# Two layers of experts in six rounds of 128 slots instead of eight, the places ranked by counts, w1 and w3 loaded two rows to a partition

## The chip, the core and the metric

The kernel runs on one core of a Trainium2 chip. A core has a matrix engine (TensorE, PE in the rows, with its weight loads as PEld), VectorE (DVE), ScalarE (ACT), GpSimd (POOL) and SyncE (SP); on SP stand the transfers from memory that this text is about. The engines have queues of their own and wait for each other through semaphores. The metric is the device time of one execution in microseconds, the median of several runs.

## The reference

A model of two blocks for 256 tokens of 1024 features, in float32. The first block has two layers; each is a mixing layer of four kinds of attention and then a mixture of experts. The second block has feed-forward, mLSTM and Mamba sublayers, which the change doesn't touch. The mixture of experts, cut to what matters:

```python
def _hier_moe(x, w_group, b_group, w_expert, b_expert, w1, w3, w2):
    g_sel = argmax(x @ w_group + b_group)                # one of 4 groups
    e_logits = (x @ w_expert + b_expert)[group g_sel]    # its 4 experts
    top_logit, top_idx = lax.top_k(e_logits, 2)
    gate = softmax(top_logit) * softmax(g_logits)[g_sel]
    ...
    h = silu(xb @ w1[e]) * (xb @ w3[e])                  # 1024 -> 512
    y = h @ w2[e]                                        # 512 -> 1024
    ...
    return sum over the two experts of a token of gate * y
```

So 256 tokens make 512 assignments to 16 experts, 32 per expert on average, and each layer needs all of w1, w3 and w2: 16 experts of 6.3 MB.

## The kernel before

**Work of a stage.** After the mixing layer, `route` (L977) works out for each token tile t (128 tokens) the two experts, the gates G and `pos`, each assignment's number among those of its expert. `moe` (L1066) then gives every expert 64 slots. A one-hot matrix `Ds` (tokens by slots, `dispatch` L1035) multiplies x, kept as two parts xh and xl, into `xe`, the slots' tokens transposed. The experts go by twos: a round p works on 128 slots, 64 of one expert and 64 of the other, so there are eight rounds. `up(p)` multiplies the slots of `xe` with w1 and then with w3, the two experts in the two column halves of TensorE (128\*64), four steps of two blocks of 128 features each; ScalarE and VectorE make h = silu(.) * (.). `down(p)` transposes h to hT, multiplies by w2 in four steps, and multiplies the result, scaled by the gate (yh and yl), with CT, the transpose of Ds, into four accumulators. The loop runs up(p) and then down(p - 1). Every second round starts with a dispatch of four experts; `collect` makes CT and the gates of eight.

**The fuller expert.** `count` (L1120), in the middle of up(0), sums the counts, and `place_fullest` (L1041) lets the fullest of experts 4 to 15 change places with the one at place TWICE = 11. That expert has 64 more slots: its pieces of w1, w3 and w2 are kept in `kept`, `select` (L1254) collects 64 more tokens after up(4), `more_up` (L1290) multiplies them after up(5), and `more_down` (L1314) follows after down(5). Assignments beyond that go into a loop behind the stage (`overflow` L1331), which runs nj times, 64 assignments each, and loads the expert's weights again.

**Weights.** `load_w` (L239) loads pieces of 512 KB, [128 partitions, h, n]. For w1 and w3 (n = 512) partition p gets rows p and p + 128 of a piece, for w2 (n = 1024) one row. An expert has four pieces each of w1, w3 and w2. `experts` (L910) yields the loads in the order of use: w1 and w3 of round p, then w2 of round p - 1. SP issues all of them in this order. A piece needs a slot of SBUF: there are 36 of 4 KB per partition (`take`, `give`), which hold everything else of that size too, and a load waits until the slot's last reader is done. The mixing layer loads ahead until 14 slots are left (`prefetch`). From expert 4 on the expert of a place is known on the chip alone: SP reads it from `who`, which place_fullest writes.

All matmuls of experts go through `mm` (L188), those of dispatch and the like through a bank's `mm` (L112). A float32 matmul is two instructions in the trace.

Of the kernel before, what the change touches and what calls it, by code (L numbers as in the profile page):

```python
# [12 lines left out]
F32R = mybir.dt.float32r  # L13
# [3 lines left out]
OP = mybir.AluOpType  # L17
# [3 lines left out]
P = 128  # L21
# [26 lines left out]
def _consts():  # L48
# [15 lines left out]
    addf("slots", np.broadcast_to(np.arange(64) + 1.0, (P, 64)))  # L64
    pos = np.arange(256, dtype=np.float32)
# [39 lines left out]
class Bank:  # L105
    """a PSUM bank that several products share as one accumulation group"""
# [18 lines left out]
class K:  # L125
# [89 lines left out]
    def copy(self, out, in_, eng=None):  # L215
        """PSUM or SBUF to SBUF, the two engines in turn."""
# [5 lines left out]
    def rstd(self, ss, scale, eps, n=1):  # L222
        """(ss * scale + eps) ** -0.5"""
# [7 lines left out]
    def rsqrt_sum(self, ss, n):  # L231
        """(ss[0] + ss[1] + n * EPS) ** -0.5: the reciprocal root mean square, over n ** 0.5"""
# [6 lines left out]
    def load_w(self, src, kt, n):  # L239
        """[kt*128, n] of DRAM, in pieces [128, h, n] of at most 512 KiB: [(first k, h, what loads it)]"""  # L240
# [28 lines left out]
    def held_back(self, eng):  # L269
        """on ScalarE or VectorE: not before what self.holds names, [how many, behind what] after each other"""  # L270
# [6 lines left out]
    def mm3(self, out, l, r, start, stop):  # L277
        """(lh + ll) (rh + rl) but for ll*rl"""
# [7 lines left out]
    def pieces(self, w, scale=None):  # L286
        """split one after the other"""
# [5 lines left out]
    def xk(self, xT, k, t=None):  # L293
        """(hi, lo) of block k of an x^T, of one token tile or both"""
# [3 lines left out]
    def rows_t(self, sp, xT, out, t, lo_last=False):  # L298
        """out = x_t @ w for one token tile; w in split pieces [128, h, n]"""
# [11 lines left out]
    def dense_rows(self, w, xT, outs):  # L311
        """outs[t] = x_t @ w for both token tiles, piece by piece"""
# [6 lines left out]
    def acc_t(self, sp, xT, acc, t, first=True, last=True):  # L319
        """acc[t][half] (+)= x_t @ w; w in split pieces [128, h, 1024]"""  # L320
# [7 lines left out]
    def dense_cols(self, w, blocks, xT):  # L328
        """for (bank, out, c, n) in blocks: out [n, 256] = (x @ w[:, c:c+n])^T"""
# [10 lines left out]
    def make_xT(self, rows, t, xT, kt=KT, r=None, k0=0, mod=None, bank=None, hold=None):  # L340
        """rows [128, kt*128] -> blocks k0 to k0 + kt of xT, token tile t, times r (of rows); mod: times and plus columns"""
# [31 lines left out]
    def load_params(self):  # L373
# [40 lines left out]
        # row vectors, on every partition  # L414
# [53 lines left out]
    def bcast(self, ap):  # L468
        """a [1024] vector on every partition"""
# [4 lines left out]
    def log1p_exp(self, pairs):  # L474
        """for (out, v): out = ln(1 + exp(-|v|)); function by function"""
# [11 lines left out]
    def mixing(self, l, xT, done):  # L487
        """x^T -> the heads' outputs -> the output projection; done(t, acc) at each token tile's end"""
# [24 lines left out]
        def evac_z(dst, ps, scale):  # L513
            """ps [128 (2 heads), 2, n] -> dst [128, 4, n], each head alone with zeros beside it"""
# [7 lines left out]
        def rope(dst, src, t, hn, half, tab):  # L522
            """src (PSUM) and dst [128, hn, 2*half]"""
# [11 lines left out]
        def softmax_pv(ss, vs, t, hs, hb, po, pov):  # L535
            """one softmax over the keys of all of ss (each [128, hb, nk]); pov[:, hs + j] += p @ [v, 1]"""
# [25 lines left out]
        def attend(scores, vs, h0, n=1):  # L562
            """scores(t, hs, hb) -> n banks of scores, [128, hb, keys] each; then the four heads' outputs"""
# [15 lines left out]
        def head_norm(pv, den, t, h0):  # L579
            """(pv / den) * (mean((pv / den)^2) + EPS)^-0.5 = pv * (mean(pv^2) + EPS den^2)^-0.5, transposed"""  # L580
# [20 lines left out]
        # -- latent attention's first projections, and the forget gates  # L601
# [33 lines left out]
        # -- stick-breaking and forgetting attention's projections  # L635
# [10 lines left out]
        def mixed(c, rv, c0):  # L646
            """512 columns: v of rv on, rows; q or k of c0 on, columns"""
# [262 lines left out]
    def experts(self, l):  # L910
# [11 lines left out]
        for p in range(9):  # L922
            for name, p, kt, n in (("w1", p, KT, 512), ("w3", p, KT, 512), ("w2", p - 1, 4, D)):
                if not 0 <= p < 8:
                    continue
# [1047 lines left out]
```

## Time and profile before

| what | value |
|---|---|
| three runs | 2217.69, 2224.88 and 2225.89 us, median 2224.88 us |
| span of the profiled execution | 2215.9 us; its own time is one of the three, 1.8 to 10.0 us above the span |
| TensorE matmuls busy | 2051.5 us, 93% |
| TensorE weight loads | 1496.1 us, 68% |
| VectorE, ScalarE, GpSimd | 1224.6, 827.2 and 85.8 us |
| moved from memory | 514.29 MB, 233 GB/s over the span |

How to read it: a busy TensorE is not one at its peak, since matmuls are pipelined and a row counts those under way. The granted clock is the share of TensorE's full clock, 1.00 for 2.4 GHz and 0.50 for 1.2 GHz. A rate of transfers means something only stage by stage, since the stages differ.

### The profile page before, as it was taken

The numbers are of one execution on the slowest core, as the hardware profiler recorded it, in microseconds if no ns is written. First come the engines' busy times: TensorE is split into PE (matmuls) and PEld (weight loads), VectorE is DVE, ScalarE is ACT, GpSimd is POOL, SyncE is SP. The second block draws the span as 40 slices with busy tenths as digits, with TensorE's granted clock in tenths as the row PEclk, the third lists the DMA queues.
The fourth block names the chain that finished last, engine by engine and source line by source line (L and its number), as shares of the span: only waits on it lengthen the run. The fifth ranks groups of instructions, "written<-read, shape, count | busy, mean of one in ns | idle before, by whom it ended". The sixth has DMA issues, their size and how long they took to land.

```text
span 2215.9 us, 28561 instructions
## 1 busy us (share of the span) xinstructions
PE 2051.5 (93%) x10572; PEld 1496.1 (68%) x10572; DVE 1224.6 (55%) x2005; ACT 827.2 (37%) x1293; POOL 85.8 (4%) x138
## 2 busy tenths in 40 slices
PE   8998899989997999959998988997999898988998
PEld 7876434438776434327786966776778797876887
DVE  5866411136876211146766875774577568655453
ACT  5543101024543110133444553444344456744442
POOL 1000000000000000000001010000000000010000
PEclk9999999999998999979999999998999999998999
DMA  7855999966756999937864955865676443244663
GB/s 245 299 158 197 331 398 398 374 216 212 256 179 221 361 394 382 400 120 253 272 230 145 315 192 192 279 226 160 219 264 233 139 143 87 88 150 124 191 189 105
DMA packets 249499, 517.29 MB, mean 233 GB/s; under 512 B 23036, under 2 KB 39434, under 8 KB 249354
## 3 DMA queue, kind: packets, MB, share of 16 engines
q1 hardware_dynamic: 249354, 515.41, 67.7%
q8 instruction: 85, 1.39, 0.3%
q14 instruction: 60, 0.49, 0.1%
HBM read 514.29 MB, written 1.05 MB: 233 GB/s over the span
## 4 chain that ended last, share of the span: by engine, by line
PE 43%; DMA 4%; DVE 4%; issue 2%; ACT 2%; POOL 0%; SPq 0%; DVEq 0%; POOLq 0%; ACTq 0%
PE ps L188 36%; PE ps L112 5%; DMA w<-in_ffn_w_dram 2%; DVE lo L261 1%; PE ps L192 1%; DMA adaw<-in_ada_w_dram 1%; ACT hi L259 1%; DMA w<-in_mb_w_in_dram 1%; DMA w<-in_mb_w_out_dram 0%; DVE xTl L366 0%; DVE u L1449 0%; DVE adac L1416 0%; DMA w<-in_ml_w_out_dram 0%; ACT xTm L363 0%; DVE x L1452 0%
## 5 line engine op out<-in xcount | busy, mean ns | idle before, releaser
L188 PE MATMUL ps<-hi,xTh 128*128 128x512 f32 (+3 forms) x1632 | 637.9, 395 | 37.8 <-ACT xTh L365 24.3
L188 PE MATMUL ps<-hi,xTl 128*128 128x512 f32 (+3 forms) x1632 | 637.4, 391 | 12.1 <-DVE xTl L366 9.6
L188 PE MATMUL ps<-lo,xTh 128*128 128x512 f32 (+3 forms) x1632 | 607.8, 387 | 8.0 <-DVE lo L261 8.0
L261 DVE TENSOR_TENSOR lo<-w,hi 128x1024 fp32r<-128x1024 f32 (+2 forms) x398 | 477.3, 1214 | 248.7 <-ACT hi L259 229.8
L259 ACT CAST hi<-w 128x1024 fp32r<-128x1024 f32 (+2 forms) x398 | 409.0, 1042 | 505.5 <-DMA w<-in_ffn_w_dram 285.3
L188 PEld LDWEIGHTS ps<-hi,xTh 128*128 128x128 f32 x1632 | 314.8, 194 | 108.6 <-ACT xTh L365 30.7
L188 PEld LDWEIGHTS ps<-hi,xTl 128*128 128x128 f32 x1632 | 315.7, 194 | 82.7 <-DVE xTl L366 16.7
L188 PEld LDWEIGHTS ps<-lo,xTh 128*128 128x128 f32 x1632 | 312.0, 191 | 75.0 <-DVE lo L261 11.6
L188 PE MATMUL ps<-w,xe 128*64 128x512 f32 x1024 | 240.9, 597 | 0.0
L1416 DVE SCALAR_TENSOR_TENSOR adac<-adaw,cact,adac 128x512 f32<-128x512 f32 x252 | 187.9, 750 | 40.2 <-DMA adaw<-in_ada_w_dram 37.0
L188 PEld LDWEIGHTS ps<-w,xe 128*64 128x64 f32 x1024 | 72.7, 136 | 137.3 <-issue 130.7
L188 PE MATMUL ps<-w,hT 128*64 128x512 f32 x488 | 119.1, 610 | 1.6 <-DVE hT L1174 1.6
L112 PE MATMUL ps<-xTh,hi 128*128 128x256 f32 x384 | 112.0, 293 | 0.6 <-DVE dr L531 0.6
L112 PE MATMUL ps<-xTh,lo 128*128 128x256 f32 x384 | 110.8, 289 | 0.0
L112 PE MATMUL ps<-xTl,hi 128*128 128x256 f32 x384 | 110.1, 288 | 0.0
L1165 DVE TENSOR_TENSOR h<-h,ps 128x512 f32<-128x512 f32 x16 | 11.0, 687 | 168.7 <-PE ps L188 168.7
L1186 ACT ACTIVATE yh<-ps,gs 128x512 fp32r<-128x512 f32 x32 | 21.5, 686 | 171.0 <-PE ps L188 166.2
L188 PEld LDWEIGHTS ps<-w,hT 128*64 128x64 f32 x488 | 39.1, 140 | 65.2 <-issue 59.1
L365 ACT CAST xTh<-ps 128x512 fp32r<-128x512 f32 (+1 forms) x84 | 42.6, 524 | 98.8 <-PE ps L192 88.2
L1187 DVE SCALAR_TENSOR_TENSOR yl<-ps,gs,yh 128x512 fp32r<-128x512 f32 x32 | 23.6, 749 | 98.4 <-ACT yh L1186 97.9
L112 PEld LDWEIGHTS ps<-xTh,hi 128*128 128x128 f32 x384 | 75.1, 196 | 1.3 <-issue 1.0
L112 PEld LDWEIGHTS ps<-xTh,lo 128*128 128x128 f32 x384 | 75.0, 195 | 0.5 <-DVE lo L261 0.2
(390 smaller groups left out, 2113.1 us busy)
## 6 DMA issues: line engine op xcount, KB each, us to landing
w<-in_w_dram SPq DMA_DIRECT2D x378, 512.0 KB
w<-in_ffn_w_dram SPq DMA_DIRECT2D x264, 512.0 KB
adaw<-in_ada_w_dram SPq DMA_DIRECT2D x144, 512.0 KB
w<-in_w_in_dram SPq DMA_DIRECT2D x60, 512.0 KB
w<-in_mb_w_in_dram SPq DMA_DIRECT2D x40, 512.0 KB
w<-in_ml_w_in_dram SPq DMA_DIRECT2D x24, 512.0 KB
w<-in_w_out_dram SPq DMA_DIRECT2D x16, 512.0 KB
w<-in_mb_w_out_dram SPq DMA_DIRECT2D x16, 512.0 KB
```

What stands on the lines that cost most here:

```text
L112: self.k.nc.tensor.matmul(out, lhsT, rhs, start=not self.started, stop=stop)
L188: self.nc.tensor.matmul(out, lhsT, rhs, start=start, stop=stop)
L192: self.nc.tensor.transpose(out, in_, self.ident[:n, :n])
L259: self.nc.scalar.copy(hi, w)
L261: self.nc.vector.tensor_sub(lo, w, hi.bitcast(F32))
L365: first = nc.scalar.copy(h, ps)
L1165: V.tensor_mul(h, h, hp[1])
L1186: nc.scalar.mul(yh, py[n], g)
L1187: V.scalar_tensor_tensor(yl, py[n], g, yh.bitcast(F32), OP.mult, OP.subtract)
L1416: nc.vector.scalar_tensor_tensor(prev, wt[:, k], cc, prev, OP.mult, OP.add)
```

## The change

The 16 places become eight of 64 slots and eight of 32 (BIG = 8). The first eight go by twos in rounds 0 to 3, the others by fours in rounds 4 and 5, each of the four in a quarter of TensorE's columns. Experts 0 to 3 keep places 0 to 3; the other twelve are ranked by count on the chip (`place_sorted`): the fullest goes to place 7, which is TWICE now, the next three to places 4 to 6, the rest to places 8 to 15. `select`, `more_up` and `more_down` come with place 7, so after up(2), up(3) and down(3). w1 and w3 are loaded by `load_w2`, in which partition p gets rows 2p and 2p + 1 of a piece; x is read with the same order (`block`). The counts that lead to `overflow` go by the new room.

```diff
+BIG = 8
-TWICE = 11  # the place of the expert that is given 64 more slots
+TWICE = 7
+ROUNDS = [tuple(range(i, i + 2)) for i in range(0, BIG, 2)] + [tuple(range(i, i + 4)) for i in range(BIG, 16, 4)]
...
+    slots = np.where(np.arange(16) < BIG, 64.0, 32.0)
+    addf("base", np.broadcast_to(slots, (P, 16)))
+    addf("cap", np.broadcast_to(slots + 64.0 * (np.arange(16) == TWICE), (P, 16)))
+    ranks = [i for i in range(FIXED, 16) if i != TWICE]
+    addf("rankof", np.broadcast_to([0.0 if i == TWICE else 1.0 + ranks.index(i) for i in range(FIXED, 16)], (P, 16 - FIXED)))
...
+    def load_w2(self, src, kt):
+        src = src.rearrange("(k p j) n -> p k j n", p=P, j=2)
+        def piece(k):
+            w = self.take([2, 512], "w")
+            self.nc.sync.dma_start(w, src[:, k])
+            return w
+        return [(2 * k, 2, lambda k=k: piece(k)) for k in range(kt // 2)]
+    @staticmethod
+    def block(x, k):
+        return x.rearrange("t (i p j) -> t i j p", p=P, j=2)[:, k // 2, k % 2]
...
     def experts(self, l):
-        for p in range(9):
-            for name, p, kt, n in (("w1", p, KT, 512), ("w3", p, KT, 512), ("w2", p - 1, 4, D)):
...
-                for i, pair in enumerate(zip(*(self.load_w(at(name, 2 * p + c), kt, n) for c in range(2)))):
+        for r in range(len(ROUNDS) + 1):
+            for name, r, kt, n in (("w1", r, KT, 512), ("w3", r, KT, 512), ("w2", r - 1, 4, D)):
...
+                load = self.load_w2 if n == 512 else lambda src, kt: self.load_w(src, kt, D)
+                for i, pieces in enumerate(zip(*(load(at(name, e), kt) for e in ROUNDS[r]))):
...
-        self.Ds.append([take([8, 64], "Ds", F32R) for q in range(2)])
+        self.Ds.append([take([8, 64 if q == 0 else 32], "Ds", F32R) for q in range(2)])
...
-    def place_fullest(self):
+    def place_sorted(self):
+        key, rank = (self.small(n, tag="fl" + t, bufs=1) for t in "kr")
+        pair, six = self.take([n, n], "flp"), self.take([6, n, n], "flx")
...
+        V.scalar_tensor_tensor(key, R[:, 4], 16.0, self.F("iota16m")[:, FIXED:], OP.mult, OP.subtract)
+        V.tensor_tensor(pair, cols(key), rows(key), OP.is_gt)
+        V.tensor_reduce(rank, pair, AX.X, OP.add)
+        V.tensor_tensor(pair, cols(rank), rows(self.F("rankof")), OP.is_equal)
+        V.tensor_tensor(six, R[:, :, None, :].to_broadcast([P, 6, n, n]), pair[:, None].to_broadcast([P, 6, n, n]), OP.mult)
+        V.tensor_reduce(R, six, AX.X, OP.add)
...
         def dispatch(q, xe, ks):
+            slots = [(d[0][:, q * 4:q * 4 + 4] if q < 2 else d[1]).rearrange("p e s -> p (e s)") for d in Ds]
...
-                            bk.mm(bk.t[:, j * 256:(j + 1) * 256], x[:, (k + j) * P:(k + j + 1) * P],
-                                  Ds[t][q // 2][:, q % 2 * 4:q % 2 * 4 + 4].rearrange("p e s -> p (e s)"), i == j == t == 1)
+                            bk.mm(bk.t[:, j * 256:(j + 1) * 256], self.block(x, k + j), slots[t], i == j == t == 1)
...
         def weights(p):
-            w = [self.weight() for _ in range(2)]
+            w = [self.weight() for _ in ROUNDS[p]]
...
         def up(p, xe):
-                        for c in range(2):
-                            s0 = (p % 2) * P + 64 * c
-                            self.mm(ps[64 * c:64 * c + 64], xe[k // 4][:, k % 4, s0:s0 + 64], w[c][:, k - k0], k == 0, k == KT - 1)
+                        for c in range(len(w)):
+                            n = P // len(w)
+                            s0 = (p % 2) * P + n * c
+                            self.mm(ps[n * c:n * c + n], xe[k // 4][:, k % 4, s0:s0 + n], w[c][:, k - k0], k == 0, k == KT - 1)
...
         def down(p, h):
-                    for c in range(2):
-                        self.mm(py[n][64 * c:64 * c + 64], hT[:, k, 64 * c:64 * c + 64], w[c][n] if type(w[c]) is list else w[c][:, 0, n * 512:(n + 1) * 512], k == 0, k == 3)
+                    for c in range(len(w)):
+                        cs = slice(P // len(w) * c, P // len(w) * (c + 1))
+                        self.mm(py[n][cs], hT[:, k, cs], w[c][n] if type(w[c]) is list else w[c][:, 0, n * 512:(n + 1) * 512], k == 0, k == 3)
...
-        for p in range(9):
+        for p in range(len(ROUNDS) + 1):
...
-            if p in (0, 4):
-                collect(p // 4)
+            if p in (0, BIG // 2 - 1):
+                collect(len(gates))
...
     def select(self, oh, base, n):
-                    bk.mm(xv[:, k], x[:, k * P:(k + 1) * P], Ds[t], k == KT - 1 and t == 1 and x is xs[-1])
+                    bk.mm(xv[:, k], self.block(x, k), Ds[t], k == KT - 1 and t == 1 and x is xs[-1])
```

## Rows read from the trace of the kernel before

**Rows 1.** The page's 40 slices of the span, in tenths busy.
```profile
PE   8998899989997999959998988997999898988998
DMA  7855999966756999937864955865676443244663
```

**Rows 2.** Stretches in us: length, busy of PE, PEld, DVE, ACT, POOL, clock, DMA share, GB/s.
```profile
252.00:386.00 134.00, 133.15 (x618) 56.93 (x615) 22.30 (x56) 11.99 (x19) 0.00 (x0) 0.96 1.04 396
363.00:374.00 11.00, 10.22 (x41) 6.82 (x42) 1.70 (x4) 1.17 (x2) 0.00 (x0) 0.53 1.05 394
386.00:404.00 18.00, 17.42 (x111) 8.86 (x110) 1.11 (x2) 0.98 (x2) 0.00 (x0) 1.00 0.90 316
404.00:460.00 56.00, 54.84 (x256) 22.24 (x258) 8.09 (x12) 5.01 (x8) 0.00 (x0) 1.00 1.03 402
460.00:487.00 27.00, 25.19 (x110) 10.01 (x106) 5.13 (x8) 4.35 (x6) 4.15 (x8) 1.00 0.39 123
868.00:886.00 18.00, 17.41 (x113) 8.94 (x112) 1.16 (x3) 0.98 (x2) 0.00 (x0) 1.00 0.97 346
```

**Rows 3.** Waits: PEld from 237 to 487 us, SP from 386 to 404 us.
```profile
PEld ps L188 <- DMA w<-in_w_dram: 2.8, 10, 0.3
...
SPq L248 <- PE ps L188: 13.5, 10, 4.2
```

**Rows 4.** Groups by form, PE and PEld, 237 to 487 us: busy, mean ns of one.
```profile
L188 PE MATMUL ps<-w,xe 128*64 128x512 f32 x512 | 121.3, 597 | 0.0
L188 PE MATMUL ps<-w,hT 128*64 128x512 f32 x244 | 60.2, 611 | 0.8 <-DVE hT L1174 0.8
...
L188 PE MATMUL ps<-yh,CT 128*128 128x512 f32 x32 | 10.7, 430 | 2.3 <-ACT yh L1186 2.3
...
L112 PE MATMUL ps<-Dt,xh 128*128 128x64 f32 x16 | 3.9, 281 | 0.0
...
L112 PEld LDWEIGHTS ps<-Ds,xh 128*128 128x128 f32 x60 | 10.0, 205 | 6.1 <-issue 4.1 <-PE ps L188 1.6 <-DVE hTo L1311 0.3
```

**Rows 5.** Timeline at 77 us: start, length, what.
```profile
76.89 0.16 PEld L188 LDWEIGHTS ps<-adac,picks 128*32 128x32 f32 x8 [0.37 <-issue]
76.89 0.43 PE L188 MATMUL ps<-adac,picks 128*32 128x128 f32 x8
```

**Rows 6.** Transfers from 290 to 306 us (w1, w3) and from 442 to 458 us (w2).
```profile
DMA packets 3241, 6.25 MB, mean 391 GB/s; under 512 B 190, under 2 KB 190, under 8 KB 3241
...
DMA packets 1789, 6.53 MB, mean 408 GB/s; under 512 B 198, under 2 KB 198, under 8 KB 1787
```

**Rows 7.** Loads issued from 60 to 390 us, and PE's groups from 237 to 390 us.
```profile
w<-in_w_dram SPq DMA_DIRECT2D x139, 512.0 KB
wh<-in_w_dram SPq DMA_DIRECT2D x6, 256.0 KB
...
L188 PE MATMUL ps<-w,xe 128*64 128x512 f32 x358 | 85.0, 598 | 0.0
L188 PE MATMUL ps<-w,hT 128*64 128x512 f32 x116 | 30.5, 627 | 0.8 <-DVE hT L1174 0.8
L188 PE MATMUL ps<-wh,hT 128*64 128x512 f32 x12 | 3.6, 598 | 0.0
```

**Rows 8.** Timeline: h of round 3, more_up, transposes, the stage's end, the next stage's start.
```profile
321.19 0.60 ACT L1164 ACTIVATE h<-ps 128x512 f32<-128x512 f32 x1 [10.88 <-PE ps L188]
...
395.85 7.49 PE L188 MATMUL ps<-w,xo 128*64 128x256 f32 x62
404.19 0.60 PE L192 MATMUL ps<-cf,h 128*128 128x128 f32 x4
...
485.64 1.08 PE L188 MATMUL ps<-yl,CT 128*128 128x512 f32 x4
492.70 1.94 PE L192 MATMUL ps<-cf,x 128*128 128x128 f32 x8 [5.98 <-DVE x L906]
```

**Rows 9.** VectorE's timeline at 250 us.
```profile
249.74 0.23 DVE L1060 TENSOR_TENSOR R<-R,sm 128x72 f32<-128x72 f32 x1
...
250.84 0.67 DVE L1038 TENSOR_TENSOR Ds<-cf,R 128x512 fp32r<-128x512 f32 x1
```

More of the change, by code (lines that the diff above doesn't have):

```diff
@@ L920, in at @@
             return A[name][l, bass.ds(who[i], 1)].rearrange("a k n -> (a k) n")
-        for p in range(9):
-            for name, p, kt, n in (("w1", p, KT, 512), ("w3", p, KT, 512), ("w2", p - 1, 4, D)):
-                if not 0 <= p < 8:
+        for r in range(len(ROUNDS) + 1):
+            for name, r, kt, n in (("w1", r, KT, 512), ("w3", r, KT, 512), ("w2", r - 1, 4, D)):
+                if not 0 <= r < len(ROUNDS):
                     continue
-                for i, pair in enumerate(zip(*(self.load_w(at(name, 2 * p + c), kt, n) for c in range(2)))):
-                    for c, (k, _, load) in enumerate(pair):
-                        if name == "w2" and p == 0 and 2 * i + c < IN_HALVES:
+                load = self.load_w2 if n == 512 else lambda src, kt: self.load_w(src, kt, D)
+                for i, pieces in enumerate(zip(*(load(at(name, e), kt) for e in ROUNDS[r]))):
+                    for c, (k, _, piece) in enumerate(pieces):
+                        if name == "w2" and r == 0 and 2 * i + c < IN_HALVES:
                             w = [self.take([512], "wh") for _ in range(2)]
@@ L933, in experts @@
                         else:
-                            yield load()
+                            yield piece()
     def prefetch(self, keep):
@@ L1044, in place_fullest @@
         V = self.nc.vector
         n = 16 - FIXED
-        R, place = self.R[:, :, FIXED:], self.R[:, :, TWICE:TWICE + 1]
-        m, oh, no, six, old = (self.small(w, tag="fl" + t, bufs=1) for t, w in (("m", 1), ("o", n), ("n", n), ("x", 6 * n), ("s", 6)))
-        i16 = self.F("iota16m")[:, FIXED:]
-        six = six.rearrange("p (a b) -> p a b", a=6)
-        each = lambda v: v[:, None, :].to_broadcast([P, 6, n])
-        V.tensor_reduce(m, R[:, 4], AX.X, OP.max)
-        V.scalar_tensor_tensor(oh, R[:, 4], m, i16, OP.is_equal, OP.mult)
@@ L1053, in place_fullest @@
[L1053 to L1061 removed]
+        R = self.R[:, :, FIXED:]
@@ L1129, in count @@
                 self.dispatch(t, 8, 16)
-            f, n1 = self.small(16, tag="f16", bufs=2), self.small(1, tag="n1", bufs=2)
-            V.tensor_scalar(f, cnt, 64.5, None, OP.is_gt)
-            V.memset(f[:, TWICE:TWICE + 1], 0.0)
-            for n in (128.5, 192.5):
-                V.scalar_tensor_tensor(f, cnt, n, f, OP.is_gt, OP.add)
+            over, f, n1 = self.small(16, tag="o16", bufs=2), self.small(16, tag="f16", bufs=2), self.small(1, tag="n1", bufs=2)
+            V.tensor_sub(over, cnt, self.F("cap"))
+            V.tensor_scalar(f, over, 0.5, None, OP.is_gt)
+            for n in (64.5, 128.5, 192.5):
+                V.scalar_tensor_tensor(f, over, n, f, OP.is_gt, OP.add)
             V.tensor_reduce(n1, f, AX.X, OP.add)
             V.tensor_copy(nj, n1[0:1])
-            V.memset(base, 64.0)
+            V.tensor_copy(base, self.F("base"))
         def weights(p):
-            w = [self.weight() for _ in range(2)]
+            w = [self.weight() for _ in ROUNDS[p]]
             if p == TWICE // 2:
@@ L1189, in down @@
                     for y in (yh, yl):
[L1190 removed]
+                        self.mm(acc[t][n], CT[t][p // 4][:, p % 4], y, p == 0 and y is yh, p == len(ROUNDS) - 1 and y is yl)
                 give(yh, yl)
@@ L1342, in overflow @@
             e = nc.values_load(ei, engines=[mybir.EngineType.SP], min_val=0, max_val=15)
-            weights = lambda n: self.load_w(A[n][l, bass.ds(e, 1)].rearrange("a k n -> (a k) n"), A[n].shape[2] // P, A[n].shape[3])
-            hT = self.more_up([weights(n) for n in ("w1", "w3")], xo)
-            self.more_down(weights("w2"), hT, cT, lambda t, n: self.ps_mm(), add=add)
+            weights = lambda n: A[n][l, bass.ds(e, 1)].rearrange("a k n -> (a k) n")
+            hT = self.more_up([self.load_w2(weights(n), KT) for n in ("w1", "w3")], xo)
+            self.more_down(self.load_w(weights("w2"), 4, D), hT, cT, lambda t, n: self.ps_mm(), add=add)
     def tick(self, n=1):
```

48 lines of the change are left out of this document (22 added, 26 removed).

## The prediction

> **What bounds the kernel now.** I read the slices first: [rows 1] show where TensorE and the transfers are both full. Two such stretches, about 240 to 490 us and 720 to 970 us, are the two expert stages; the diff changes no other stage, so the rest of the span moves with their ends. The table by stretches [rows 2] cuts the first: from 252 to 460 us TensorE is busy throughout and the transfers run at 396 to 402 GB/s, except for 386 to 404 us, where they fall to 316 GB/s. After 460 us they fall to 123 GB/s: the experts' last weights are in, and TensorE still works for 27 us on them. So two limits lie close together, and the stage ends with TensorE. The waits confirm it [rows 3]: TensorE's weight loads wait for w only 2.8 us in 250, while SP, which issues every load in order, waits 13.5 of the 18 us from 386 to 404 for matmuls to free a slot.
>
> **What TensorE no longer does.** A stage has 512 matmul instructions w x xe and 256 w x hT, of which 12 read wh [rows 4, 7]: 121.3 + 60.2 + 3.6 = 185.1 us busy, over 8 rounds 23.1 us a round. The products with CT are 32 of yh, 10.7 us [rows 4], and as many of yl: some 2.7 us a round, so a round costs 25.8 us. Six rounds instead of eight take away 2 x 25.8 = 52 us per stage, 103 us in all, if a round of four experts costs what one of two costs. The 128*32 form is in the trace already: eight picks matmuls, two for each of four column groups, are over in 0.43 us [rows 5]. Four transposes of 128 columns, which go one after another, take 0.60 us [rows 8], about 0.3 for one and 0.1 for each more. Eight would take 1.0 us one after another, 0.6 two abreast, 0.4 four abreast; the row is nearest to four. So I take a step of four experts at the price of a step of two, 1.8 us (15.2 us / 8); above, at two at a time, 3.6 us.
>
> **What the transfers still do.** An expert still brings 12 pieces of 0.524 MB, 192 a stage. The pieces of w1 and w3 are 2 KB packets now, those of w2 4 KB: a stretch of the first ran at 391 GB/s, one of the second at 408 GB/s [rows 6], so a piece takes 1.34 or 1.285 us. With two neighbouring rows on a partition all should be of the second kind. Where the transfers bind that is 0.055 us a piece, for 52 pieces of w1 and w3 (below) 3 us per stage; where TensorE binds it is nothing.
>
> The Trainium skill (DMA: Bandwidth & Descriptors, Specifications) puts line rate at 512 B and more for a transfer, by which 2 KB rows gain nothing from becoming 4 KB. The trace's 391 against 408 GB/s disagrees; by the rule the sum below would be 3 us smaller per stage.
>
> A round of two wants 24 pieces, 31 us of transfers against 25.8 us of TensorE, a round of four 48 pieces, 62 us against 25.8. So TensorE waits in the last two rounds, and the stage ends when the transfers do. What matters is when they stop before.
>
> **Where they stop.** By 390 us, in the stall, SP had issued 139 + 6/2 = 142 pieces, and TensorE had used (358 + 116 + 12)/4 = 121.5, four instructions a piece [rows 7]. With the five of place TWICE kept till then, 26 pieces were held. That is the room for weights. The stall falls where the extra slots' work adds to the round: select's 32 matmuls (16 of xh, 3.9 us [rows 4], and 16 of xl between them, some 4 us together), part of it at a granted clock of 0.53, that is 1.2 GHz [rows 2], then more_up, 7.5 us [rows 8]. In the change TWICE is 7, so this comes in rounds 2 and 3, and there the transfers are still far ahead. Rounds 0 to 3 go as before: their h is at 321.2 us [rows 8], w3 of round 3 ends 7.6 us later, at 329, select brings that to 333, and more_up ends at 341; half the 5 us that the slow clock cost, 343. When more_up starts, TensorE has used the 64 pieces of w1 and w3 of four rounds and the 16 of w2 of two; eight are kept, so 72 slots have come free, and 72 + 26 = 98 pieces are issued. The other 94 go from about 337 us on (more_up frees one about every 1 us), at 1.285 us: 121 us. Collect and the tail of down between them cost another 4 us. That makes 462 us, where before the last piece was in at 460.
>
> **The sum.** Behind the last piece TensorE has one step (1.8, or 3.6 us at 1.2 GHz), the scaling and eight products with CT: 4.5 to 9 us by the rows of the last round [rows 8], I take 7.5. The stage ends at 469.5 instead of 485.64 + 1.08 = 486.7 us [rows 8]: 17 us earlier. The second stage has the same shape (the same dip, at 868 to 886 us [rows 2]), so 17 us again: 34 us of the possible 103. The profiled span of 2215.9 us becomes 2182 us. The three runs listed lie 1.8 to 10.0 us above that span, their median 9.0; carried over, 2224.9 - 34 = 2191 us.
>
> What the next stage needs hides: in the last rounds slots are free, so its loads stand right behind the experts' in SP's queue, and the rest of the stage with the layer norm (6.0 us of idle TensorE [rows 8]) covers four pieces at 1.285 us. Uncovered, they would cost 5 us a stage. Behind TensorE's new waits for w stand its own next steps alone; ScalarE and VectorE wait for these as before, and SP for none of them.
>
> The sort in place of the swap: a VectorE operation of 72 elements takes 0.23 us, one of 512 0.67 us [rows 9], about 1.0 ns an element. Three of 144 elements (0.30 each), two of 864 (1.02 each) and one of 12 make 3.2 us, where the swap's eleven, none over 72 elements, took at most 0.23 each, 2.5 us. SP's first load for a ranked place comes that 0.7 us later, while pieces issued before it, 1.3 us each, are still in flight. I cost it at nothing; uncovered 0.7 us a stage. The two tiles it takes from the slots and the smaller Ds and CT change a slot or two: 1.3 us each way per slot.
>
> Reading x as stationary with a step of two elements has no row; the loads of xh take 0.2 us now [rows 4] and run beside other matmuls. Below, nothing; above, twice as long, 0.2 us each on the 96 of dispatch and select ahead of the end of more_up: 19 us per stage. Nearest is the row as it stands, so I take nothing.
>
> The Trainium skill (TensorE: Matmul & The Clock Gate, Loop structure matters more than you think) warns that a wait for DMA between bursts of matmuls makes TensorE go cold. The trace grants 0.53 in a stretch of small matmuls [rows 2]; by the rule the last two rounds run at 1.2 GHz, hidden at 52 us of work in 62 us of transfers, and only the last step and products are longer.
>
> **Rivals.** (a) The transfers hardly stop, because extras and freed slots interleave better than I draw it. Then the stage ends with the stream itself: of 208 us from 252 to 460 two thirds become 4% shorter, 5.6 us, so 454 us plus 7.5: 25 us per stage, 2175 us. For it: before, the rate fell for 18 us only. Against: there the lead was smaller. (b) The four groups share TensorE two at a time: no work is saved, the stage ends at 487 as before, 2225 us. Against it [rows 5]. (c) Strided loads cost 19 us per stage: 469.5 + 19 = 488.5, 2228 us. (d) Slower: a place of 32 slots overflows. By the reference's router on its default inputs the fifth largest count outside places 0 to 3 is 32 in both layers, exactly the room. One token more, and the loop behind the stage runs once: 12 pieces from an empty queue (15.4 us), select and more_up (12 us), more_down (16 instructions at 0.24 us, 4 us), about 31 us with nothing beside it. In one layer this leaves 2222 us; from one in both on it is slower, 2191 + 62 = 2253 us.
>
> **How the numbers follow.** Forecast, transfers stopping once and then binding (20 to 45 us gained): 0.62. (a) 0.13. (b) 0.07. (c) 0.06. (d) 0.05, mostly slower. Between forecast and no change, with a longer stop or an uncovered start: 0.07. The likeliest gives 2191 us. The range runs from (a), with another 5 us for a slot or two, 2170, to 2214, a longer stop. Half a per cent, 11 us, is about what a measurement tells from no change. Faster by more: 0.62 + 0.13 + most of the last, 0.80; within: (b), part of (c) and of (d), 0.12; slower 0.08.
>
> **What the profile after would show.** Right: a dip of the transfers in the 20 us before 345 us, then 405 GB/s or more to about 460; 4 KB packets; TensorE's waits for w of over 50 us in the last two rounds; groups of four 128*32 matmuls starting within some 10 ns; both stages 15 to 20 us shorter; no overflow instructions. The sum falls if the dip is much longer than 10 us or missing, if 128*32 steps take over 3 us at full clock, or if xh loads lengthen.

## The result, and the profile after

The changed kernel takes 2189.48 us (median of 4 runs, 2184.65 to 2193.25), the kernel before 2221.61 us beside it: a ratio of 0.9852, 95% interval 0.9831 to 0.9874. That is 32 us faster, where 34 us and 2191 us were forecast. The profiled execution of after has a span of 2182.8 us and a time of its own of 2184.65 us; against the span before of 2215.9 us it is 33.1 us shorter.

The page's slices of the kernel after, TensorE and transfers, answer to [rows 1]. Digit by digit they read nearly as before; a slice of 55 us is too coarse to show what the stages lost, so I read that from stretches.

```profile
PE   7998899989997999959998989996999898988998
DMA  7855899977655999958747858764776442334663
```

The table by stretches after answers to [rows 2]; the columns are the same (length, busy of PE, PEld, DVE, ACT, POOL, clock, DMA share, GB/s).

```profile
252.00:327.00 75.00, 74.11 (x358) 32.84 (x356) 13.06 (x43) 8.05 (x12) 0.00 (x0) 0.95 1.03 411
327.00:339.00 12.00, 12.00 (x76) 5.66 (x73) 3.27 (x5) 0.60 (x1) 0.00 (x0) 1.00 0.62 204
339.00:462.00 123.00, 118.34 (x579) 39.48 (x576) 12.52 (x22) 7.26 (x12) 3.11 (x6) 0.99 1.01 402
462.00:468.00 6.00, 5.88 (x19) 2.17 (x17) 2.15 (x4) 1.38 (x2) 1.04 (x2) 1.00 1.04 395
788.00:800.00 12.00, 12.00 (x61) 4.74 (x61) 3.23 (x5) 0.60 (x1) 0.00 (x0) 1.00 0.66 227
```

Read the last column. The transfers run at 411 GB/s, fall to 204 for 12 us, and come back until 462 us. The stretch of 27 us at 123 GB/s that ended the stage before, with TensorE at work on weights long landed, is gone. The second stage has its dip at 788 us. Set against 411 GB/s, 204 over 12 us loses 6.0 us and 402 over 123 us another 2.7: by this estimate the stop costs the first stage 8.7 us.

The waits of after from 237 us to the stage's end answer to [rows 3]: the first row is TensorE's weight loads, the second SP waiting for matmuls to free a slot.

```profile
PEld ps L197 <- DMA w<-in_w_dram: 24.3, 47, 1.2
...
SPq L268 <- PE ps L197: 38.8, 33, 7.0
```

The groups by form, 237 to 475 us, answer to [rows 4].

```profile
L197 PE MATMUL ps<-w,xe 128*64 128x512 f32 x256 | 58.8, 596 | 0.0
L197 PE MATMUL ps<-w,xe 128*32 128x512 f32 x256 | 42.6, 597 | 2.6 <-DMA w<-in_w_dram 2.6
L197 PE MATMUL ps<-w,hT 128*32 128x512 f32 x128 | 37.9, 598 | 0.4 <-DVE h L1192 0.4
...
L121 PEld LDWEIGHTS ps<-Ds,xh 128*128 128x128 f32 x44 | 7.8, 222 | 3.3 <-issue 1.6 <-PE ps L197 1.6
```

Of w x xe the old form (128\*64) and the new one (128\*32) have 256 instructions each here, for eight experts each, and the mean length of one is the same (some 597 ns). What changed is how many run beside each other. Where no weight is awaited, from 398.5 to 404.5 us, the groups read:

```profile
L197 PE MATMUL ps<-w,xe 128*32 128x512 f32 x48 | 5.6, 594 | 0.0
```

48 in 5.6 us is 0.117 us each, where the form of two takes 58.8 / 256 = 0.23. Over the whole stage the new form takes 42.6 / 256 = 0.17 us, because in most of it the pieces come in one at a time. The timeline of TensorE at 415 us shows that:

```profile
414.49 0.59 PE L197 MATMUL ps<-w,xe 128*32 128x512 f32 x1
415.32 1.04 PE L197 MATMUL ps<-w,xe 128*32 128x512 f32 x2 [0.23 <-DMA w<-in_w_dram]
416.61 1.04 PE L197 MATMUL ps<-w,xe 128*32 128x512 f32 x2 [0.24 <-DMA w<-in_w_dram]
417.88 2.33 PE L197 MATMUL ps<-w,xe 128*32 128x512 f32 x12 [0.23 <-DMA w<-in_w_dram]
```

Two instructions every 1.28 us, the time of one piece: TensorE counts as busy and yet waits for the transfers. Last, the timeline of the kernel after answers to [rows 8]: h of round 3, more_up, the last steps, and TensorE's restart behind the first and the second stage.

```profile
328.91 0.60 ACT L1191 ACTIVATE h<-ps 128x512 f32<-128x512 f32 x1 [9.88 <-PE ps L197]
...
335.15 7.49 PE L197 MATMUL ps<-w,xo 128*64 128x256 f32 x62
...
463.67 0.14 PEld L197 LDWEIGHTS ps<-w,hT 128*32 128x32 f32 x2 [0.28 <-DMA w<-in_w_dram]
...
466.93 1.09 PE L197 MATMUL ps<-yl,CT 128*128 128x512 f32 x4
474.01 1.30 PE L201 MATMUL ps<-cf,x 128*128 128x128 f32 x5 [5.99 <-DVE x L931]
...
929.79 1.09 PE L197 MATMUL ps<-yl,CT 128*128 128x512 f32 x4
954.14 1.94 PE L201 MATMUL ps<-cf,rr 128*128 128x128 f32 x8 [23.26 <-DVE rr L374]
```

The last weight that TensorE waits for is there at 463.7 us and the stage ends at 468.0, where before it was 486.7: 18.7 us earlier, and all of it is kept at the restart (474.0 for 492.7). The second stage ends at 930.9 for 967.5 before, so it gained another 17.9. Behind it, though, TensorE stands idle for 23.26 us. The kernel before reads there:

```profile
966.37 1.09 PE L188 MATMUL ps<-yl,CT 128*128 128x512 f32 x4
987.01 1.94 PE L192 MATMUL ps<-cf,rr 128*128 128x128 f32 x8 [19.56 <-DVE rr L349]
```

So 3.7 us of the gain went into that idle time: -18.7 - 17.9 + 3.7 = -32.9 of the span's -33.1 us.

### The profile page after: what moved, and what is told of

Same layout as the page of the kernel before. It is cut to its first block, busy times and chain, and to the rows that moved or that the text cites. A ratio compares the mean times of both kernels' runs of the same rounds, so it can differ in the third digit from the quotient of the medians.

```text
span 2182.8 us, 28213 instructions
## 1 busy us (share of the span) xinstructions
PE 2009.1 (92%) x10436; PEld 1457.2 (67%) x10436; DVE 1213.9 (56%) x1981; ACT 817.2 (37%) x1277; POOL 84.0 (4%) x138
## 4 chain that ended last, share of the span: by engine, by line
PE 42%; DMA 5%; DVE 4%; ACT 2%; issue 2%; POOL 0%; SPq 0%; DVEq 0%; POOLq 0%; ACTq 0%
PE ps L197 36%; PE ps L121 5%; DMA w<-in_ffn_w_dram 3%; PE ps L201 1%; DVE lo L286 1%; DMA w<-in_mb_w_in_dram 1%; ACT hi L284 1%; DVE adac L1444 1%; DMA adaw<-in_ada_w_dram 1%; DMA w<-in_mb_w_out_dram 0%; DVE xTl L391 0%; DMA w<-in_ml_w_in_dram 0%; DVE x L1480 0%; ACT L1827 0%; DVE lo L290 0%
## 5 line engine op out<-in xcount | busy, mean ns | idle before, releaser
L197 PE MATMUL ps<-w,xe 128*64 128x512 f32 (+1 forms) x1024 | 203.4, 597 | 5.3 <-DMA w<-in_w_dram 5.3
L197 PEld LDWEIGHTS ps<-w,xe 128*64 128x64 f32 (+1 forms) x1024 | 55.5, 123 | 132.1 <-issue 95.1
L197 PE MATMUL ps<-w,hT 128*32 128x512 f32 (+1 forms) x488 | 137.8, 619 | 2.4 <-issue 1.7
L197 PEld LDWEIGHTS ps<-w,hT 128*32 128x32 f32 (+1 forms) x488 | 40.3, 127 | 88.7 <-issue 70.5
L1214 ACT ACTIVATE yh<-ps,gs 128x512 fp32r<-128x512 f32 x24 | 16.5, 688 | 207.5 <-PE ps L197 207.0
L1215 DVE SCALAR_TENSOR_TENSOR yl<-ps,gs,yh 128x512 fp32r<-128x512 f32 x24 | 18.0, 750 | 123.9 <-ACT yh L1214 123.0
```

The source lines that it names most:

```text
L197: self.nc.tensor.matmul(out, lhsT, rhs, start=start, stop=stop)
L1214: nc.scalar.mul(yh, py[n], g)
L1215: V.scalar_tensor_tensor(yl, py[n], g, yh.bitcast(F32), OP.mult, OP.subtract)
```

## The experiments

The first stage of these kernels begins at 241 to 249 us in their traces, although none changes anything ahead of it. So where a few us count, I compare the length of a stage, from its first w x xe matmul to the end of its last yl x CT matmul. It is 244.7 and 242.3 us before, 225.4 and 224.5 after (first and second stage). Each length comes from one profiled execution; kernels below whose stages hold the same instructions differ by up to 1.1 us, so a single difference of 1 us means nothing.

**The reshaped loads alone.** The kernel before with two rows to a partition:

```diff
-  for i, pair in enumerate(zip(*(self.load_w(at(name, 2 * p + c), kt, n) for c in range(2)))):
+  load = self.load_w2 if n == 512 else lambda src, kt: self.load_w(src, kt, D)
+  for i, pair in enumerate(zip(*(load(at(name, 2 * p + c), kt) for c in range(2)))):
...
-  bk.mm(..., x[:, (k + j) * P:(k + j + 1) * P], ...)
+  bk.mm(..., self.block(x, k + j), ...)
```

> The kernel before with one part of the change alone: w1 and w3 are loaded two rows to a partition (4 KB packets) and x is read with a step of two; eight rounds of two, the places and the swap are as before. My theory: each expert stage of the kernel before ends with TensorE, some 20 us behind the last weights, so faster pieces are worth nothing: within 0.3% of the kernel before, about 2221 us, the stages ending within 2 us of 486.7 and 967.5 us, and the dip of the transfers only becomes deeper. Rival: the transfers bound the stage before, and the reshape is a main part of the gain: 5 to 6 us earlier per stage, about 2210 us. Rival: strided loads of x cost: up to 19 us later per stage, about 2260 us.

Measured: 2221.11 us, ratio to before 1.0018 (1.0001 to 1.0035); stages of 245.0 and 243.2 us. Nothing is gained, although the transfers were faster. The table by stretches, laid on the same places as [rows 2] (this stage began 6.5 us later):

```profile
259.00:393.00 134.00, 133.16 (x617) 57.83 (x614) 21.79 (x50) 12.00 (x19) 0.00 (x0) 0.96 1.01 402
393.00:411.00 18.00, 17.42 (x112) 8.90 (x111) 1.11 (x2) 0.98 (x2) 0.00 (x0) 1.00 0.80 279
```

402 GB/s ahead of the dip instead of 396, and 279 in it instead of 316: what the faster pieces win they lose in the dip. The stage before was bound by TensorE.

**The rounds without the reshaped loads.** The kernel after with load_w for w1 and w3 and contiguous blocks of x:

```diff
-  load = self.load_w2 if n == 512 else lambda src, kt: self.load_w(src, kt, D)
+  load = lambda src, kt, n=n: self.load_w(src, kt, n)
...
-  bk.mm(..., self.block(x, k + j), ...)
+  bk.mm(..., x[:, (k + j) * P:(k + j + 1) * P], ...)
...
```

> The kernel after without one part: w1 and w3 are loaded one row to a partition again (2 KB packets) and x is read in contiguous blocks; the six rounds and the sort stay. My theory: the stage ends with the transfers, and 52 to 96 pieces of w1 and w3 lie where they bind, so it ends 3 to 5 us later per stage: 6 to 10 us more than the kernel after, 2195 to 2200 us. Rival, the size of a packet makes no difference: 2189 us. Rival, the reshape is most of the gain: above 2205 us.

Measured: 2187.0 us, ratio 0.9865 (0.9847 to 0.9883), stages of 227.3 and 226.7 us: 1.9 and 2.3 us longer than after. The time misses the 2195 to 2200 us that were expected: it can't tell 4 us from nothing, and only the stages show them. A stretch of w1 and w3 and one of w2, by the table of stretches of this run, then the first of them in the kernel after:

```profile
378.00:418.00 40.00, 37.21 (x175) 10.47 (x175) 2.88 (x4) 1.97 (x3) 0.00 (x0) 1.00 1.05 389
424.00:462.00 38.00, 37.52 (x132) 11.13 (x131) 2.88 (x4) 1.37 (x2) 3.11 (x6) 1.00 1.03 411
...
378.00:418.00 40.00, 37.92 (x176) 10.61 (x178) 3.57 (x5) 1.97 (x3) 0.00 (x0) 1.00 1.03 410
```

389 GB/s against 410: the smaller packet is slower here too, where the transfers bind, and costs some 2 us a stage. It costs no more, it seems, because slower transfers get less far ahead and are stopped less: from 327 to 339 us this run moves 322 GB/s, after 204.

**Without the 64 extra slots.**

```diff
   if p == TWICE // 2:
-      kept.append(w[TWICE % 2])
+      pass
...
-  cT, xo = self.select(oh, base, "0")
...
-  hT = self.more_up([pieces(kept[o:o + 4], 2) for o in (0, 4)], xo)
...
-  self.more_down(pieces(kept[8:], 1), hT, cT, lambda t, n: acc[t][n], False)
```

> The kernel after without the 64 extra slots of place TWICE: select, more_up and more_down are left out and no piece is kept for them, so the assignments past 64 of that expert are not computed. My theory: the transfers stop in rounds 2 and 3 because these 15 to 20 us of TensorE work run while the room for weights is full and eight pieces are kept; without them the dip at 327 to 339 us goes, and the stage still ends with the transfers, 8 to 12 us earlier per stage: 2165 to 2173 us. Rival, TensorE's own work sets the end: all the work left out is gained, 20 us or more per stage, below 2150 us. Rival, the dip comes from something else: less than 3 us per stage, above 2183 us.

Measured: 2168.29 us, ratio 0.9779 (0.9761 to 0.9797), stages of 217.9 and 216.5 us: 7.5 and 7.9 us shorter. Some 20 us of TensorE's work left out of a stage bring 8. The dip is gone:

```profile
327.00:339.00 12.00, 12.00 (x52) 4.31 (x49) 1.44 (x2) 1.27 (x2) 0.00 (x0) 1.00 1.03 410
339.00:455.00 116.00, 109.33 (x471) 31.15 (x468) 8.49 (x12) 5.21 (x8) 3.11 (x6) 1.00 1.03 411
```

**More work for TensorE in the rounds of four**, in two runs. First each matmul right behind its original:

```diff
+  for r in range(2 if n == 32 else 1):
-      self.mm(ps[...], xe[...], w[c][:, k - k0], k == 0, k == KT - 1)
+      self.mm(ps[...], xe[...], w[c][:, k - k0], k == 0 and r == 0, k == KT - 1 and bool(r or n == 64))
...
```

> The kernel after with each matmul of w1, w3 and w2 in the two rounds of four issued twice, so that these products are added up twice and the result is another one. That is about 23 us more of TensorE per round if four groups run abreast, 46 us per stage. My theory: in these rounds TensorE waits for the transfers (26 us of work in 62 us), so the copies fall into the waits; the last step is 2 us longer, and the work that TensorE is behind with when round 4 begins takes some us longer to clear: 2 to 6 us per stage, 2193 to 2202 us. Rival, TensorE sets the end as before: 40 us or more per stage, above 2265 us.

then with the copies behind all four groups of a step:

```diff
+  for r in range(R):
       for c in range(len(w)):
           self.mm(..., k == r == 0, k == KT - 1 and r == R - 1)
...
```

> As the run that doubled the matmuls of the rounds of four, but with the copies behind all four column groups of a step and not each behind its original, so that four groups can still run abreast (0.107 us per instruction, where the trace of that run shows w x hT in pairs, 0.215 us per instruction). The 384 copies per stage are 41 us more of TensorE at 0.107 us. These products are again added up twice. My theory: in the rounds of four TensorE waits for the transfers, and the copies fall into the waits: 2 to 10 us longer per stage, 2194 to 2210 us. Rival, TensorE has next to no slack and the stage is bound by both: 30 us or more per stage, above 2250 us.

Measured: 2323.67 us (ratio 1.0492, 1.0469 to 1.0515) and 2267.8 us (1.0245, 1.0212 to 1.0277). These times say little, since the doubled products change the second layer's routing and the overflow loop runs behind its stage. The stages tell the two apart: 258.0 and 258.8 us in the first run, 32.7 and 34.3 more than after; 230.4 and 228.9 in the second, 5.0 and 4.5 more, which is what was expected of a stage (the time expected of it, 2194 to 2210 us, left out that loop). What was expected of the first run was wrong in the price of a copy. The groups by form for w x hT, from 472 to 484 us of the first run:

```profile
L197 PE MATMUL ps<-w,hT 128*32 128x512 f32 x58 | 12.8, 595 | 0.0
```

and from 460 to 466 us of the second:

```profile
L197 PE MATMUL ps<-w,hT 128*32 128x512 f32 x60 | 6.7, 593 | 0.0
```

0.22 us each against 0.112: behind its original, a copy of w x hT makes two run abreast instead of four, as if it had to wait for the column group. That this is the cause is not shown: over the stage w x xe, in the same order, took 0.117 us in the first run and 0.113 in the second. The groups of the second run over its first stage:

```profile
L197 PE MATMUL ps<-w,xe 128*32 128x512 f32 x512 | 57.8, 593 | 0.0
L197 PE MATMUL ps<-w,hT 128*32 128x512 f32 x256 | 32.9, 594 | 0.0
```

w x hT takes 58.4 us in the first run for these 32.9, which is most of the 27.7 us between their stages. By the estimate 384 x 0.112 = 43 us the second run's copies add that much to TensorE's work, and the stage is 5 us longer. TensorE's waits for w, 22.5 us from 360 to 475 us after, are down to 1.7:

```profile
PEld ps L197 <- DMA w<-in_w_dram: 1.7, 6, 0.3
```

So some 38 us per stage were slack.

**Four slots less.**

```diff
+  if p == 1:
+      away = [self.free[UNIT].popleft() for _ in range(4)]
...
+  self.free[UNIT].extend(away)
```

> The kernel after with four slots of 4 KB per partition taken out of use from the second round of a stage to its end. My theory: the stop of the transfers begins when the room for weights is full, so each slot less is a piece less that is under way before more_up frees some: 1.285 us per slot, 4 to 6 us later per stage, 2197 to 2202 us. Rival, the stop is set by SP's wait for something else than room: 2187 to 2192 us.

Measured: 2202.86 us, ratio 0.9925 (0.9904 to 0.9946), stages of 228.7 and 230.3 us: 3.3 and 5.9 us longer, 1.1 us per slot. From 252 to 327 us the transfers now run at 402 GB/s, from 327 to 339 us at 325: the stop begins earlier and is spread. The time is just above the 2197 to 2202 us expected. The stages hold 9 us of it; the profiled run shows 4.4 more ahead of the first stage, where the edit does nothing, and the rest behind it, most of it behind the second.

**One overflow in each layer.**

```diff
+  slots[8] = 31.0
   addf("base", np.broadcast_to(slots, (P, 16)))
```

> The kernel after with 31 instead of 32 slots told to the count and the overflow for place 8, the fullest of the places of 32. If that place holds exactly 32 assignments, as the reference's router gives it in both layers, the loop behind the stage runs once in each layer for one assignment, which is then added twice. It prices the rival that did not happen. My estimate: 31 us per layer, 62 us in all: 2251 us, slower than the kernel before. Rival, part of it hides beside the loads and the norm of the next stage: 15 to 25 us per layer, 2220 to 2240 us. If the place holds fewer than 32, 2189 us.

Measured: 2260.78 us, ratio 1.0181 (1.014 to 1.0221), 71 us above after. From the start of the first stage to that of the second it is 503.3 us, after 463.8: 39.6 us for one pass instead of 31. TensorE's timeline of the pass:

```profile
473.81 4.37 PE L122 MATMUL ps<-Dt,x 128*128 128x64 f32 x20
...
481.51 9.82 PE L198 MATMUL ps<-w,xo 128*64 128x256 f32 x64 [0.68 <-ACT xo L230]
...
496.29 1.08 PE L198 MATMUL ps<-w,hTo 128*64 128x512 f32 x4 [0.15 <-DMA w<-in_w_dram]
498.17 1.13 PE L198 MATMUL ps<-yo,cT 64*128 64x512 f32 x4 [0.79 <-DVE yo L230]
...
508.42 1.94 PE L202 MATMUL ps<-cf,x 128*128 128x128 f32 x8 [5.68 <-DVE x L932]
```

The next stage's first matmul comes 33.3 us later behind the stage's end than after. Of the other 6, 5.4 lie between there and the second stage, in a part of the kernel whose further loads SP issues from 503.86 us on, behind the loop's; that these loads are what makes it longer is read from their order, not tested.

**Without the branch**, for the 3.7 us at the second stage:

```diff
-  v = nc.values_load(nj, min_val=0, max_val=15)
...
-  with tc.If(v > 0):
-      self.overflow(l, v, cnt, base, ss)
...
```

> The kernel after without the branch behind each expert stage and the loop in it (the overflow, which did not run in the kernel after, is left out). It tests where the 3.7 us went that the second stage gained and TensorE's restart behind it did not show: 23.3 us of idle TensorE there, 19.6 before. My theory: TensorE's branch took 6.2 us at 930.4 us (0.4 us before), and GpSimd's first instruction of the next stage waits for it; without the branch the idle is 20 us or less, 3 to 6 us gained there, little at the other stage, 2183 to 2186 us. Rival, the delay is GpSimd's own (some 8 us between its broadcast and its power): the idle stays 22 to 24 us, 2189 us.

Measured: 2181.57 us, ratio 0.9833 (0.9806 to 0.9859), just under the 2183 to 2186 us expected. The stages are as after (225.5 and 223.4 us), TensorE's idle time behind them is 5.5 and 18.36 us. GpSimd's timeline behind the second stage, which ends here at 931.1 us:

```profile
932.55 1.80 POOL L1447 PARTITION_BROADCAST gate<-modg  x4 [237.01 <-DMA w<-in_ffn_w_dram]
941.82 0.59 POOL L237 TENSOR_TENSOR sm<-sm,cf 128x1 f32<-128x1 f32 x1 [7.47 <-issue]
```

and after, where it ends at 930.9:

```profile
936.94 1.80 POOL L1454 PARTITION_BROADCAST gate<-modg  x4 [241.93 <-DMA w<-in_ffn_w_dram]
946.48 0.59 POOL L237 TENSOR_TENSOR sm<-sm,cf 128x1 f32<-128x1 f32 x1 [7.73 <-issue]
```

The broadcast comes 1.4 us behind the stage without the branch, 6.1 with it, and the norm's power 9.3 and 9.5 us later. (The releaser named, a load, is not what held the broadcast.)

**Another order of the same rounds**, in two runs. First the fours in the middle, TWICE in the fifth round:

```diff
+TWICE = 5
+ROUNDS = [(0, 1), (2, 3), (8, 9, 10, 11), (12, 13, 14, 15), (4, 5), (6, 7)]
...
```

> The kernel after with the rounds in another order: two rounds of two, the two rounds of four, two rounds of two; the place with 64 more slots is the first of the last two (place 5), so select runs in the second round of four, more_up and more_down in the last two. Same work, same bytes. My theory: the extras come when TensorE has just waited for the transfers and holds nothing but the eight kept pieces, so the transfers do not stop, and the dip at 327 to 339 us goes: the weights are in some 7 us earlier per stage. The last two rounds with more_up and more_down are about 63 us of TensorE beside 62 us of transfers, so part of that may be lost at the end: 3 to 7 us earlier per stage, 2175 to 2183 us. Rival, the stop is not tied to where the extras run: 2187 to 2192 us. Rival, TensorE's last rounds set the end: 5 us or more later per stage, above 2199 us.

Measured: 2177.66 us, ratio 0.9832 (0.9809 to 0.9856). The dip is gone (409 GB/s from 327 to 339 us, 411 behind), but the stages, 223.5 and 223.2 us, are only 1.8 and 1.2 us shorter, where 3 to 7 were expected. TensorE's timeline says why:

```profile
451.63 1.46 PE L200 MATMUL ps<-w,hTo 128*64 128x512 f32 x6
...
458.32 5.37 PE L200 MATMUL ps<-w,hT 128*64 128x512 f32 x22
463.65 1.56 PE L200 MATMUL ps<-yh,CT 128*128 128x512 f32 x4
```

The transfers had fallen to 192 GB/s from 456 us on, and TensorE was still at more_down and the last round of two, without a wait for w. (The rest of the gain is the idle time behind the second stage, 19.78 us.) So the second run ends on a round of four:

```diff
+TWICE = 4
+ROUNDS = [(0, 1), (2, 3), (8, 9, 10, 11), (4, 5), (6, 7), (12, 13, 14, 15)]
...
```

> The kernel after with the order two, two, four, two, two, four: one round of four between the pairs and the other at the end; the place with 64 more slots is the first of the third pair (place 4). Same work, same bytes. The order two, two, four, four, two, two had no dip of the transfers, its weights were in at 455.5 us, but TensorE ended 10.5 us later, with more_down and two rounds of two behind the stream. My theory: with the extras beside a round of four and TensorE waiting again in the last round, the transfers do not stop and TensorE ends 5 to 6 us behind them: 461 us, 7 us earlier per stage than the kernel after, 2172 to 2177 us. Rival, the end is set by how TensorE's last round comes in and not by the stop: within 3 us of 468 us, 2183 to 2190 us.

Measured: 2172.04 us, ratio 0.9798 (0.9773 to 0.9823), stages of 217.6 and 216.7 us, 7.8 us shorter each: nearly all that the stop had cost, and as much as leaving out the extras had given.

```profile
327.00:339.00 12.00, 11.88 (x50) 4.11 (x47) 1.50 (x2) 1.38 (x2) 0.00 (x0) 1.00 1.03 408
339.00:455.00 116.00, 110.82 (x556) 39.52 (x553) 11.65 (x21) 6.57 (x11) 3.12 (x6) 0.99 1.03 411
```

**The gate ahead of the branch**, on top of that order:

```diff
   for p in range(len(ROUNDS) + 1):
+      if l == 1 and p == len(ROUNDS):
+          self.gate_rows(0)
+          nc.gpsimd.tensor_tensor(self.small(1, tag="pw"), self.F("slots")[:, :1], self.gate[:, :1], OP.pow)
...
-  self.gate_rows(3 * i + 2 * j)
+  if 3 * i + 2 * j:
+      self.gate_rows(3 * i + 2 * j)
```

> The kernel with the order two, two, four, two, two, four, and in its second layer GpSimd's broadcast of the next sublayer's gate, with one power behind it that brings back what the norm needs, is issued ahead of the last round's down and so ahead of the branch, not behind it. It tells apart what the 23.7 us of idle TensorE behind the second stage are made of. My theory: the branch of TensorE, the broadcast that waits for it and the 7.7 us of GpSimd between the broadcast and the norm's power stand in one chain; ahead of the branch the last two are hidden, and the idle falls to 6 to 13 us (6.0 at the first stage, where no gate is made), 2160 to 2168 us. Rival, the norm waits for something else behind the branch, such as its loads: the idle stays above 18 us, 2170 us or more.

Measured: 2160.09 us, ratio 0.9735 (0.9708 to 0.9762). The idle time behind the second stage is 11.96 us instead of 23.65. This is the fastest version, with all of the reference's work done.

## Why the prediction was right, step by step

**What bounds the stage: right.** Faster transfers alone brought nothing before (1.0018). After, TensorE has some 38 us to spare per stage, and the stage ends 4.3 us behind the last weight that TensorE waits for.

**A step of four at the price of one of two: right, but worth less than it looks.** 0.112 to 0.117 us an instruction was taken as 1.8 us / 16 = 0.1125. (15.2 / 8 is 1.9 and not 1.8, which changes nothing.) The four of a group start within 20 ns, at 398.77 to 398.79 us. The picks row [rows 5] had carried it, and by this price rival (b) is out.

What (b) would have cost, though, was wrong: no gain at all, 2225 us. The second run with copies has its very condition. There the rounds of four take TensorE 57.8 + 32.9 = 90.7 us, about what the rounds of two take for as many experts (58.8 of w x xe, 29.3 of w x hT, 3.6 of wh). Still its stage is only 5 us longer than after, and 14 shorter than before. The products with CT fall with the number of rounds however many groups run abreast (yh and yl: 10.7 + 10.3 us before, 8.6 + 7.8 after), and the prediction's own 2.7 us a round say so. So does a dispatch less, which the sum left out; before and after:

```profile
L112 PE MATMUL ps<-Ds,xh 128*128 128x256 f32 x60 | 13.8, 314 | 0.1
...
L121 PE MATMUL ps<-Ds,xh 128*128 128x256 f32 x44 | 10.3, 324 | 0.0
```

(xl: 13.1 and 9.6 us.) By this stand-in, four abreast in place of two are worth some 5 of the 19 us that the first stage gained.

**Where the transfers stop: right in place and sum, not in shape.** Drawn was one dip of about 10 us ahead of 345 us. There is a main one at 327 to 339 us and smaller ones behind it, 8.7 us in all in the first stage. By 337 us SP had issued 98 whole pieces and 6 halves, 101 for the forecast's 98: at 330 us TensorE had used 74 of 96, eight of them kept, so the room is some 30 pieces and not 26. The extras beside a full room are the cause: without them, or with the same extras where the transfers are behind, 7.5 to 8 us come back; and each slot taken away costs 1.1 us, forecast 1.3. Rival (a), hardly a stop, is out, and its 454 us plus a tail, 461.5, are about what the better order reaches (460.1).

**The end: right, in part by luck.** The last piece was forecast for 462 us and is there at 463.7; behind it 7.5 us were taken, and 4.3 are used, since the other pieces of the last step have been used when its last one lands. The two errors, 1.7 us and 3.2 the other way, partly cancel: 469.5 was forecast, 468.0 measured.

**4 KB packets: right in kind, 3 us forecast, 1.9 and 2.3 measured per stage.** (Behind the forecast's stop 54 pieces of w1 and w3 are left, not 52; the sum stays 3 us.) 389 against 410 GB/s stands against the rule of the Trainium skill (DMA: Bandwidth & Descriptors, Specifications) that puts line rate at 512 B: by that rule the run without the reshaped loads would have had stages as long as after.

**What was costed at nothing.** The sort takes 248.42 to 251.82 us, 3.4 us, forecast 3.2, and nothing waited for it that the transfers did not cover. Loads of x with a step of two take 222 ns a piece for 205 before and 210 without the step: rival (c) is out. No place overflowed, so rival (d) is out as well; it would have cost 39.6 us and not 31 in the first layer: 33 up to the next stage's first matmul, and 5 more behind it, where the next stage's loads stand behind the loop's in SP's queue, which the sum left out.

**The next stage's start: wrong for the second stage, by 3.7 us.** Its idle time was taken as unchanged. It hangs on a chain that the prediction did not look at: TensorE's branch, GpSimd's broadcast of the gate, 6.7 to 8.8 us on GpSimd, the norm's power. Behind the second stage TensorE's branch past the loop, which did not run, took 6.2 us; before it took 0.43. The rows of this branch, shortest, median and longest of both stages in ns, after and before:

```profile
L1252 PEldq COMPARE_BRANCH  x2: 353/3280/6207, 467.7 to 930.4; - x2
...
L1224 PEldq COMPARE_BRANCH  x2: 352/390/427, 486.5 to 967.0; - x2
```

Take the branch away and 4.9 us come back; move the rest of the chain ahead of it and 11.7 do. So the branch and the chain are shown as the cause of the 3.7 us. The two stages gained 36.6 us where 34 were forecast; that this loss brings the total so near to the forecast is luck. Why the branch is longer stays open. Behind the second stage it takes 6.0 to 6.2 us after and in five of the variants, with the next sublayer's loads at 353 GB/s after (925 to 937 us), and 0.3 to 0.4 us before, with the reshaped loads alone and with the fours in the middle (195 GB/s around it before and with the fours in the middle). But behind the first stage of after it took 0.35 us right behind 395 GB/s (462 to 468 us), so a high rate ahead of it does not make it long; there the transfers fell to 119 GB/s in the next 6 us. What goes with the length in all nine of these kernels is a transfer of instructions. From 930.4 to 936.6 us, within the long branch of after, the queues read:

```profile
q8 instruction: 1, 0.02, 1.1%
```

In each long branch one such transfer of q8 runs, in no short one; another follows 0.6 to 0.8 us behind the end of each branch of the second stage, long or short. No run tested whether the branch waits for it.

**TensorE's waits of over 50 us: not so.** The row reads 24.3 us. The wait is there, 38 us by the doubled copies, but pieces land one at a time, and a matmul of one column group alone counts as busy.

**The clock.** In the first stage of after it fell to half speed twice: 0.57 from 305 to 313 us, in select, as before in [rows 2], and 0.50 from 347 to 350 us, behind the small matmuls of 343 to 347 us. From 350 to 473 us it was granted in full, with nearly all of TensorE's waits for w (22.5 of 24.3 us from 360 us on):

```profile
350.00:473.00 123.00, 114.70 (x538) 35.24 (x534) 16.34 (x29) 11.86 (x16) 5.28 (x10) 1.00 0.99 390
```

The Trainium skill (TensorE: Matmul & The Clock Gate, Loop structure matters more than you think) warns of a long wait for DMA between matmuls. The prediction read from it that the last two rounds would run cold, and they did not: here the waits are many and short (47 of them, the longest for w 1.2 us).

## What to carry to other kernels

When two limits lie close together, taking work from one buys only the distance to the other: 52 us less of TensorE's work per stage, as forecast, became 18 to 19 us (with 43 of them put back, 14 us were still gained), and the faster loads, worth 2 us after, were worth nothing before. Once a stream of transfers sets the end, look for every place where it stops, and put work that holds buffers beside stretches in which the stream is behind anyway: the order of six rounds was worth 8 us per stage with not one instruction less. And follow the chain past the stage's end: a stage that ends earlier meets other transfers, and what stood hidden behind its tail, here a branch and a broadcast on GpSimd, becomes part of the path.

## What the runs showed of the hardware that was not expected

A TensorE branch past a loop that did not run lasted 0.3 to 0.4 us in some places and 6.0 to 6.2 us in others; one transfer of instructions ran within each long one, and none within a short one. On GpSimd, 6.7 to 8.8 us pass between a partition broadcast and the next power, with nothing that the profile shows to wait for. Matmuls of 32 columns ran four abreast at 0.112 to 0.117 us; with each group's instruction twice in a row w x hT fell to 0.22 us, and w x xe stayed at 0.117.
